# Transfers of an attention stage: from a written order with short lead to the scheduler's order with longer lead

## The chip, the cores and the metric

The kernel runs on one core of one Trainium2 chip. The metric is the device time of one execution in microseconds; the median over several runs is compared. TensorE is called PE, VectorE DVE, ScalarE ACT, GpSimd POOL, SyncE SP. Almost all transfers are issued from SP's queue.

## What is computed

One inference step of an encoder layer, for 1024 frames of a new stream and 32 frames of a running one with 512 cached frames (1056 token columns, model width 1024, 16 heads of 64). The reference, cut to its core:

```python
h = rmsnorm(x, norm_g)
q = rmsnorm(h @ Wq per head, q_g) * 64 ** -0.5
k = rmsnorm(h @ Wk per head, k_g);  v = h @ Wv
logf = log_sigmoid(h @ Wf + b_f);   C = cumsum(logf)
o = softmax(causal(q k^T + C[t] - C[s])) v            # per head
u = (h @ Wua) * sigmoid(h @ Wub);   conv = depthwise31(u) + b_dw
ya = (o * silu(h @ Wga)) @ w_pa
yb = (silu(layernorm(conv)) * silu(h @ Wgb)) @ w_pb
y = x + (sigmoid(h @ Wma) * ya + sigmoid(h @ Wmb) * yb) @ w_out
```

All data are 32-bit floats. Products are made in three passes over a high and a low part of each operand.

## The kernel before

**Stages.** The kernel runs through four stages. The opening transposes and scales the tokens (`x_split`) while it makes the first projection. The projections follow: V, the conv input `u`, keys and queries, and the gates `ga`; their results go to scratch tensors in device memory (`s_q`, `s_k`, `s_v`, `s_ga`, ...). Then comes the attention, head by head, and last the three output projections.

**A projection's weights** come as raw tiles of 512 KB in batches of two (`Batch`). The planner `begin` starts at the first product of a batch and puts its jobs on a list by steps; a step (`beat`) is one k-tile of a product, three matmuls. Jobs: the squares of the raw tile (`stage`, L117), the sum over partitions (`total`), the power of two to scale by (`power`), the high part by ACT (`split`) and the low part by DVE (`rest`, tile `wl`, L141). The next batch's raw tiles are loaded by `after.load` (L109), at steps 17 and 27. The raw tiles have four buffers, so a load waits until DVE has read the tile that lay there.

**The opening.** `x_split(0, ...)` goes over eight k-tiles: transposes on PE (L573), high part by ACT, low part by DVE (`xl`, L576), then the jobs listed for that k-tile, then the products of the two first weights, which lag behind (`drain`). `total(2)` sums the squares of the second weight on PE (L477) after its squares on ACT (`top(1)`, L596); `known(1)` makes its scale, `high(1, 0)` and `low(1, 0)` split its first third. `rooted(2, 3)` makes the square roots for tokens of tiles 2 to 4.

**The attention.** The list `seq` holds 16 heads of eight query blocks each, and four `Sample` entries for the running stream. At turn n of the loop over `seq`, PE makes the scores of block n + 3 (`start`, L1094 and L1095), transposes the softmax of block n (`turn`, L1119), goes four steps further in the remaining gate projections (`fill`, matmuls at L183 into `pj`, evicted by ACT into one of three tiles `t`, L932, and stored, L933), and makes the values of block n - 2. A head's values are made once, at its last block (L1138). Between are DVE (mask, maximum), ACT (exponential) and POOL (division). Conv taps of the last two channel groups run on DVE meanwhile.

**A head's operands.** `Head.load` issues eight transfers into QB, KB, QA and KA (L948 to L955), two buffers each, 1.5 MB in all. `Head.load_v` (L962) loads V, 256 KB, one buffer. Head 0 is loaded during the last gate projections ahead of the attention. In the loop the load of a head stands where its first block is five entries ahead, so two turns ahead of its first scores; V stands behind the values of the head before, which is the last reader of the one buffer.

**What sets the order.** Under `tc.manual_schedule` the engines named in it run their instructions as written; the others are ordered by a scheduler at build time, from a simulated timeline. In the opening and the projections PE, DVE and ACT follow the written order and SP doesn't. In the attention it is PE and SP (L986), in the last stage PE alone at first. Each engine's queue is in order: an instruction that waits holds up what is behind it.

Of the kernel before, what the change touches and what calls it, by code (L numbers as in the profile page):

```python
# [8 lines left out]
F32 = mybir.dt.float32  # L9
# [13 lines left out]
H = 16  # L23
# [30 lines left out]
def build(tc, xT, xt, wv, wf, ckT, cv, clT, stT, vec, cst, yT, kT, vO, lfO, cpT, csT):  # L54
# [4 lines left out]
    def pool(name, bufs=1, stack=es, **kw):  # L59
        return stack.enter_context(tc.tile_pool(name=name, bufs=bufs, reuse_waits="tile", **kw))  # L60
# [29 lines left out]
    class Batch:  # L90
# [31 lines left out]
        def total(self):  # L122
            pool, tag = totals[-1]
            self.ps = pool.tile([128, 512], F32, name="tot", tag=tag)
            if self.n == 2:
                nc.tensor.matmul(self.ps[:, :2], ones_b, self.topb, start=True, stop=True)
            else:
                for i in range(2):
                    nc.tensor.matmul(self.ps[:, 0:1], ones_b, self.topb[:, i:i + 1], start=(i == 0), stop=(i == 1))
# [7 lines left out]
        def high(self, i, wh, raw, ks):  # L137
            nc.scalar.mul(wh[:, ks, :], raw[:, ks, :], self.s[:, i:i + 1])  # L138

        def low(self, i, wl, wh, raw, ks):  # L140
            nc.vector.scalar_tensor_tensor(wl[:, ks, :], raw[:, ks, :], self.s[:, i:i + 1], wh[:, ks, :],  # L141
                                           op0=ALU.mult, op1=ALU.subtract)
# [78 lines left out]
    def begin():  # L221

        if not plan:
            return
        b = plan.pop(0)
        after = plan[0] if plan else None
        t = pace["tick"]
        jobs = [(25, b.total), (27, b.power)]
        if b.n == 2:
            jobs += [(3, lambda: b.stage(0)), (13, lambda: b.stage(1))]  # L230
            for i, n in ((0, 29), (1, 39)):
                jobs.append((n, lambda i=i: b.split(i)))
                jobs += [(n + 1 + 2 * p, lambda i=i, p=p: b.rest(i, p)) for p in range(3)]
        else:
            jobs += [(3 + 10 * i, lambda i=i: b.stage(i)) for i in range(2)]
            jobs.append((29, lambda: split.__setitem__(b.keys[0], split_v(b.keys[0][1], b))))
        if after:
            jobs += [(17 + 10 * i, after.load) for i in range(after.n)]
        prep.extend((t + n, fn) for n, fn in sorted(jobs, key=lambda e: e[0]))

    def steps(key, rh, rl, pspool, evac):
# [38 lines left out]
    class Banks:  # L280

        n = 0
# [157 lines left out]
    E = mybir.EngineType  # L440
# [72 lines left out]
    def squares(t, act=True, sl=slice(0, D), acc=None):  # L513
        r = rows(t)
        acc = rs9[:r, t:t + 1] if acc is None else acc
        sq = xip.tile([128, D], F32, name="sq", tag="sq", bufs=2)[:r, sl]
        x = xtok[t][:r, sl]
        if act:
            nc.scalar.activation(sq, x, AF.Square, accum_out=acc)
        else:  # L520
            nc.vector.scalar_tensor_tensor(sq, x, 1.0, x, op0=ALU.mult, op1=ALU.mult, accum_out=acc)

    def root(t0, nt):

        rs = rs9[:, t0:t0 + nt]
        v, y = [xip.tile([128, 4], F32, name=f"n4{i}", tag=f"n4{i}", bufs=2)[:, :nt] for i in range(2)]
        nc.vector.tensor_scalar(v, rs, 1.0 / D, EPS, op0=ALU.mult, op1=ALU.add)
        nc.scalar.activation(y, v, AF.Ln)
        nc.scalar.activation(y, y, AF.Exp, scale=-0.5)
        return lambda: newton(rs, v, y)  # L530

    def scale(t, h, pool=False):
        r = rows(t)
        x, f = xtok[t][:r, half[h]], rs9[:r, t:t + 1]
        if pool:
            nc.gpsimd.tensor_scalar(x, x, f, 1.0, op0=ALU.mult, op1=ALU.mult)
        else:
            nc.vector.tensor_scalar(x, x, f, None, op0=ALU.mult)
# [60 lines left out]
    def known(i):  # L599
        recs[i].power(psq[:, i + 1:i + 2], 1)  # L600
# [23 lines left out]
    def rooted(t0, nt):  # L624
        steps_of[t0] = root(t0, nt)
# [12 lines left out]
    for f in range(8):  # L638
# [14 lines left out]
    x_split(0, ws0, u0, {  # L653
        0: [lambda: top(1), lambda: squares(2, False)],
        1: [lambda: squares(3)],
        2: [lambda: total(2), lambda: high(0, 1), lambda: low(0, 1)],
        3: [lambda: known(1), lambda: squares(4, False), lambda: high(1, 0), lambda: low(1, 0)],
        4: [lambda: rooted(2, 3), lambda: high(0, 2)],
        5: [lambda: steps_of[2](), lambda: scale(2, 0), lambda: scale(3, 0, True), lambda: scale(4, 0), lambda: low(0, 2)],
        6: [lambda: scale(3, 1, True), lambda: scale(2, 1), lambda: high(1, 1), lambda: low(1, 1)],  # L660
        7: [lambda: scale(4, 1), lambda: high(1, 2), lambda: low(1, 2)]})
# [38 lines left out]
    def split_v(c, rec):  # L700
        wh2, wl2, raws2 = [], [], rec.raws
        for raw in raws2:
            with tc.high_priority(offset=1500):
                wh, wl = [vp.tile([128, 4, VC], F16, name=a, tag=a, bufs=4) for a in ("vwh", "vwl")]
                rec.high(0, wh, raw, slice(0, 4))
                for k in (0, 2):
                    rec.low(0, wl, wh, raw, slice(k, k + 2))
            wh2.append(wh)
            wl2.append(wl)

        def running():
            ps = pj.tile([128, 512], F32, name="pjs", tag="pj")
            for n in range(2):
                for j in range(4):
                    nc.tensor.matmul(ps[32 * j:32 * j + 32, :VC], xsm[:, 2 * j + n, :],
                                     raws2[j // 2][:, (2 * j + n) % 4, :], start=(n == 0), stop=(n == 1))
            pace["credit"] -= 1.3
            later(4, lambda: gathered(ps))

        def gathered(ps):  # L720
            v4 = vp.tile([TS, 4, VC], F32, name="v4", tag="v4", bufs=1)
            for j in range(4):
                nc.scalar.copy(v4[:, j, :], ps[32 * j:32 * j + 32, :VC])
            vs = vp.tile([TS, VC], F32, name="vs", tag="vs", bufs=1)
            nc.vector.tensor_reduce(vs, v4.rearrange("p j n -> p n j"), axis=AX.X, op=ALU.add)
            nc.vector.tensor_copy(z[:TS, 8, 4 * c:4 * c + 4], vs[:, 256:])
            nc.sync.dma_start(vO[T:, 256 * c:256 * c + 256], vs[:, :256])
            nc.sync.dma_start(s_vs[:, 256 * c:256 * c + 256], vs[:, :256])

        later(14, running)  # L730
        return wh2, wl2, rec.inv
# [4 lines left out]
    for c in range(4):  # L736
# [13 lines left out]
        pace["rate"] = R_V  # L750
        wh2, wl2, inv = split.pop(("v", c))
        begin()
        for t in range(8):
            ps = pj.tile([128, 512], F32, name="pjv", tag="pj")
            n = 0
# [181 lines left out]
    class Head:  # L937
# [20 lines left out]

        def load_v(self):
            h = self.h  # L960
            self.V = hp.tile([128, 8, 64], F32, name="V", tag="V", bufs=1)
            nc.sync.dma_start(self.V, s_v[:, :, 64 * h:64 * h + 64].rearrange("b t d -> t b d"))  # L962

    pace["rate"] = R_U
# [3 lines left out]
    hp = pool("hp", 2, stack=p2, side="right")  # L968
    heads = [Head(h) for h in range(H)]
# [13 lines left out]


    pe = ExitStack()
    pe.enter_context(tc.manual_schedule(engines={E.PE, E.SP}))  # L986
    pace["rate"], pace["credit"] = R_A, 0.0
    taps.extend(sums(7))
    psS = pool("psS", 2, stack=p2, space=PS)
# [11 lines left out]
    def fill(n):  # L1001
        for _ in range(n):
            next(flow, None)
# [145 lines left out]
    seq = []  # L1149
# [5 lines left out]
    def start(b):  # L1155
        if getattr(b, "i", 1) == 0:
            h = b.head
            if h.h % 2 == 0:
                h.ot = heads[h.h + 1].ot = ap.tile([128, T], F32, name="ot", tag="ot", bufs=2)
        b.scores()  # L1160

    def pending(b):
        return isinstance(b, Sample) or b.i % 2
# [36 lines left out]
    ln = layernorm()  # L1200
    sides["shift"] = ap.tile([128, TT], F32, name="shift", bufs=1)
    nc.sync.dma_start(sides["shift"], s_m)
    start(seq[0])
    fill(8)
    start(seq[1])
# [2 lines left out]
    for n, b in enumerate(seq):  # L1208
        if n + 3 < len(seq):
            start(seq[n + 3])  # L1210
        if n + 5 < len(seq) and getattr(seq[n + 5], "i", 1) == 0:
            seq[n + 5].head.load()
        if n + 6 < len(seq) and isinstance(seq[n + 6], Sample):
            seq[n + 6].load()
        if isinstance(b, Sample):
            fill(4)
            b.turn()
        else:
            b.turn()
            fill(4 if b.i > 2 or b.head.h != 8 else 0)  # L1220
        if n >= 2 and pending(seq[n - 2]):
            seq[n - 2].values()
        if n >= 3 and isinstance(seq[n - 3], Sample):
            seq[n - 3].finish()
        if n >= 2 and getattr(seq[n - 2], "i", 0) == 7 and seq[n - 2].head.h + 1 < H:
            heads[seq[n - 2].head.h + 1].load_v()
        if "ready" in sides:
            next(ln, None)
    for b in seq[-2:]:
# [6 lines left out]
    pe = ExitStack()  # L1236
# [9 lines left out]
    class Banks3:  # L1246
        n = 0
# [383 lines left out]
```

## Time and profile before

| | us |
|---|---|
| median of 3 runs | 1451.53 |
| lowest to highest | 1445.54 to 1453.81 |
| profiled execution | 1445.9 |
| its span, first to last instruction | 1443.9 |

| engine | busy us | share of the span |
|---|---|---|
| PE | 1347.8 | 93% |
| DVE | 976.5 | 68% |
| ACT | 723.0 | 50% |
| POOL | 496.5 | 34% |

The mean granted clock of TensorE is 0.969. The stages lie about at 0 to 60 us (opening), 60 to 560 (projections), 560 to 1160 (attention) and 1160 to 1444 (output projections). Busy shares are averages over these stages; a stage's own limit is read from its rows. In a row of waits stand the total, the number and the longest, in microseconds; in a row of the timeline the start, the length, the engine, the line, and in brackets the idle time before and what ended it.

### The profile page before, as it was taken

Reading aid. Unit: us, or ns where it says so; the run is one execution under the profiler, and the core shown is the slowest. Engines: PE = TensorE matmul, PEld = TensorE weight load, DVE = VectorE, ACT = ScalarE, POOL = GpSimd, SP = SyncE. Lnnn points to the kernel's source line nnn. Section 1 sums busy time; section 2 is a strip of 40 time slices with the busy share of each in tenths; the row PEclk is TensorE's granted clock in tenths of the full one; section 3 lists DMA queues with packets and bytes.
Section 4 is the critical chain, followed back from the end, with each engine's and each line's share of the span. In section 5 each row is a group of like instructions: output and inputs, shape, how many; then the busy total and the mean of one; then the engine's idle time right before and its main releaser. Section 6 shows DMA issues by size and latency. Waiting matters only on the chain.

```text
span 1443.9 us, 24762 instructions
## 1 busy us (share of the span) xinstructions
PE 1347.8 (93%) x9383; PEld 1020.0 (71%) x9383; DVE 976.5 (68%) x1534; ACT 723.0 (50%) x1360; POOL 496.5 (34%) x548
## 2 busy tenths in 40 slices
PE   8999999999999999787989788978888999999999
PEld 5687866666666666565666566656665689999999
DVE  6787888869798988656767645544444459455664
ACT  6544547575768535444544454534543465423321
POOL 2000126265748302333333322211211228545653
PEclk9999999999999999999999999999999999999999
DMA  6242434373435232335343543453444197743462
GB/s 233 92 148 85 125 89 130 109 195 116 131 121 168 100 128 95 99 102 148 108 130 107 155 116 83 121 149 88 116 116 124 49 359 258 233 135 120 144 202 73
DMA packets 113495, 194.96 MB, mean 135 GB/s; under 512 B 34080, under 2 KB 80032, under 8 KB 113376
## 3 DMA queue, kind: packets, MB, share of 16 engines
q1 hardware_dynamic: 113232, 193.31, 43.9%
q8 instruction: 74, 1.21, 0.4%
q14 instruction: 45, 0.37, 0.1%
q10 hardware_dynamic: 144, 0.07, 0.0%
HBM read 127.68 MB, written 65.64 MB: 134 GB/s over the span
## 4 chain that ended last, share of the span: by engine, by line
PE 71%; DMA 10%; DVE 5%; SPq 5%; ACT 4%; issue 3%; POOL 1%; ACTq 0%; DVEq 0%; POOLq 0%
PE pj L183 47%; PE pjv L760 6%; PE pj L1463 5%; PE po L1138 5%; DMA KA<-s_ak 5%; PE ptr L1119 3%; DMA raw<-wf 2%; DMA KA<-s_k 2%; PE psS L1095 1%; DVE y L368 1%; PE psS L1094 1%; ACT t L932 1%; DVE nm L1099 1%; DVE wl L141 1%; ACT P L1102 1%
## 5 line engine op out<-in xcount | busy, mean ns | idle before, releaser
L183 PE MATMUL pj<-xh,wh 128*128 128x352 f16 (+2 forms) x1536 | 489.0, 318 | 8.2 <-ACT t L932 6.9
L183 PE MATMUL pj<-xh,wl 128*128 128x352 f16 (+2 forms) x1536 | 488.1, 318 | 0.7 <-DVE wl L141 0.6
L183 PE MATMUL pj<-xl,wh 128*128 128x352 f16 (+2 forms) x1536 | 487.5, 317 | 0.1
L183 PEld LDWEIGHTS <-wh 128*128 128x128 f16 x3072 | 305.4, 99 | 165.4 <-issue 2.6
L368 DVE SCALAR_TENSOR_TENSOR y<-u,vec_t,y 128x1086 f32<-128x1086 f32 x240 | 342.6, 1428 | 9.5 <-ACT y L365 6.6
L1105 POOL TENSOR_SCALAR P<-P,nm 128x128 f32<-128x128 f32 (+7 forms) x128 | 119.1, 931 | 336.7 <-DVE nm L1104 281.7
L183 PEld LDWEIGHTS <-wl 128*128 128x128 f16 x1536 | 152.6, 99 | 84.4 <-issue 10.7
L141 DVE SCALAR_TENSOR_TENSOR wl<-raw,sc,wh 128x384 f16<-128x384 f32 (+1 forms) x192 | 119.1, 655 | 30.5 <-ACT wh L138 30.5
L1122 ACT COPY pt<-ptr 128x512 f32<-128x512 f32 (+3 forms) x128 | 64.4, 503 | 143.9 <-PE ptr L1119 143.3
L1102 ACT ACTIVATE P<-psS,nm 128x128 f32<-128x128 f32 (+7 forms) x128 | 94.8, 741 | 65.5 <-DVE nm L1099 52.0
L1094 PE MATMUL psS<-KB,QB 128*128 128x256 f32 (+2 forms) x192 | 82.7, 432 | 39.7 <-DMA KB<-s_k 33.8
L1097 DVE TENSOR_TENSOR psS<-psS,cmask 128x128 f32<-128x128 f32 x128 | 37.7, 295 | 118.2 <-PE psS L1095 117.7
L1099 DVE TENSOR_REDUCE nm<-psS 128x1 f32<-128x128 f32 (+7 forms) x128 | 96.3, 754 | 8.5 <-DVE psS L1097 0.5
L1095 PE MATMUL psS<-KA,QA 68*128 68x256 f32 (+2 forms) x192 | 70.1, 366 | 30.1 <-DMA KA<-s_ak 24.6
L1119 PE MATMUL ptr<-ident,P 128*128 128x128 f32 x576 | 93.6, 294 | 1.2 <-ACT pt L1122 1.2
L175 POOL TENSOR_TENSOR wl<-raw,wh 128x384 fp32r<-128x384 f32 (+1 forms) x51 | 63.4, 1271 | 74.6 <-ACT wh L172 58.7
L1119 PEld LDWEIGHTS ptr<-ident,P 128*128 128x128 f32 x576 | 77.2, 153 | 6.9 <-ACT pt L1122 1.5
L1094 PEld LDWEIGHTS psS<-KB,QB 128*128 128x128 f32 x192 | 37.5, 195 | 57.3 <-issue 39.9
L138 ACT ACTIVATE wh<-raw,sc 128x1024 f16<-128x1024 f32 (+1 forms) x68 | 72.7, 1089 | 7.8 <-DVE sc L158 7.5
L869 POOL TENSOR_TENSOR sql<-sqf,sqh 128x352 fp32r<-128x352 f32 x48 | 58.7, 1224 | 50.7 <-ACT sqh L866 50.6
L1138 PE MATMUL po<-pt,V 128*64 128x256 f32 x640 | 72.8, 382 | 0.3 <-ACT pts L1051 0.3
L117 ACT ACTIVATE junk<-raw 128x1024 bf16<-128x1024 f32 x62 | 65.2, 1052 | 12.9 <-DMA raw<-wf 12.8
(271 smaller groups left out, 2574.8 us busy)
## 6 DMA issues: line engine op xcount, KB each, us to landing
raw<-wf SPq DMA_DIRECT2D x92, 512.0 KB
QB<-s_q SPq DMA_DIRECT2D x32, 256.0 KB
KB<-s_k SPq DMA_DIRECT2D x32, 256.0 KB
kT<-qn SPq DMA_DIRECT2D x8, 528.0 KB
s_ga<-t SPq DMA_DIRECT2D x24, 176.0 KB
s_gb<-t SPq DMA_DIRECT2D x24, 176.0 KB
s_ma<-t SPq DMA_DIRECT2D x24, 176.0 KB
s_mb<-t SPq DMA_DIRECT2D x24, 176.0 KB
```

Source lines behind the costliest of these rows:

```text
L138: nc.scalar.mul(wh[:, ks, :], raw[:, ks, :], self.s[:, i:i + 1])
L141: nc.vector.scalar_tensor_tensor(wl[:, ks, :], raw[:, ks, :], self.s[:, i:i + 1], wh[:, ks, :], op0=ALU.mult, op1=ALU.subtract)
L183: nc.tensor.matmul(ps, a[:, kt, :], b(kt, sl), start=(first and n == 0), stop=(last and n == N - 1))
L368: t = nc.vector.scalar_tensor_tensor(y, u[:, i:i + CW], w, y, op0=ALU.mult, op1=ALU.add)
L760: nc.tensor.matmul(ps[:, :VC], a, b, start=(n == 0), stop=(n == 23))
L1094: nc.tensor.matmul(ps[:, b, :wm], QB[:, qsl], KB[:, ksl], start=True, stop=False)
L1095: nc.tensor.matmul(ps[:, b, :wm], QA[:, qsl], KA[:, ksl], start=False, stop=True)
L1099: nc.vector.tensor_reduce(nm[:, 0:1], ps[:, :nb, :w], axis=AX.XY, op=ALU.max, negate=True)
L1102: nc.scalar.activation(P[:, :nk].rearrange("p (b w) -> p b w", b=nb), ps[:, :nb, :w], AF.Exp, bias=nm[:, 0:1], accum_out=nm[:, 1:2])
L1105: nc.gpsimd.tensor_scalar(P[:, :nk], P[:, :nk], nm[:, 2:3], 1.0, op0=ALU.mult, op1=ALU.mult)
L1119: nc.tensor.transpose(pt[:, 128 * j:128 * j + 128], P[:, 128 * (4 * u + j):128 * (4 * u + j) + 128], ident)
L1138: nc.tensor.matmul(po[rows], V[:, j, :], parts[c][:, j, :], start=(c % 2 == 0 and j < 2), stop=(c % 2 == 1 and j >= 2 * c))
```

## The change

Five edits. SP leaves the written order in the attention. A head's queries and keys are loaded nine entries ahead of its first block, with head 1's ahead of the first block of all. V has two buffers, and the next head's V is loaded at block 3. The next batch's raw weights are listed at steps 5 and 15. In the opening, the sum of the second weight's squares moves from k-tile 2 to 3, its scale and first split from 3 to 4, behind the square roots.

```diff
@@ begin
-            jobs += [(17 + 10 * i, after.load) for i in range(after.n)]
+            jobs += [(5 + 10 * i, after.load) for i in range(after.n)]
@@ x_split(0, ...)
-        2: [lambda: total(2), lambda: high(0, 1), lambda: low(0, 1)],
-        3: [lambda: known(1), lambda: squares(4, False), lambda: high(1, 0), lambda: low(1, 0)],
-        4: [lambda: rooted(2, 3), lambda: high(0, 2)],
+        2: [lambda: high(0, 1), lambda: low(0, 1)],
+        3: [lambda: total(2), lambda: squares(4, False)],
+        4: [lambda: known(1), lambda: rooted(2, 3), lambda: high(1, 0), lambda: low(1, 0), lambda: high(0, 2)],
@@ Head.load_v
-            self.V = hp.tile([128, 8, 64], F32, name="V", tag="V", bufs=1)
+            self.V = hp.tile([128, 8, 64], F32, name="V", tag="V", bufs=2)
@@ attention
-    pe.enter_context(tc.manual_schedule(engines={E.PE, E.SP}))
+    pe.enter_context(tc.manual_schedule(engines={E.PE}))
...
+    heads[1].load()
     start(seq[0])
...
-        if n + 5 < len(seq) and getattr(seq[n + 5], "i", 1) == 0:
-            seq[n + 5].head.load()
+        if n + 9 < len(seq) and getattr(seq[n + 9], "i", 1) == 0:
+            seq[n + 9].head.load()
         if n + 6 < len(seq) and isinstance(seq[n + 6], Sample):
             seq[n + 6].load()
+        if getattr(b, "i", 0) == 3 and b.head.h + 1 < H:
+            heads[b.head.h + 1].load_v()
...
-        if n >= 2 and getattr(seq[n - 2], "i", 0) == 7 and seq[n - 2].head.h + 1 < H:
-            heads[seq[n - 2].head.h + 1].load_v()
```

## The prediction

> **What bounds the kernel now.** I read the page first: its span and the chain of work that ended last.
>
> ```profile
> span 1443.9 us, 24762 instructions
> PE 71%; DMA 10%; DVE 5%; SPq 5%; ACT 4%; issue 3%; POOL 1%; ACTq 0%; DVEq 0%; POOLq 0%
> ```
>
> TensorE carries the chain, but a tenth of it is transfers. The view of busy time by stretches says in which stage: opening, projections, attention, output projections. Columns: stretch, length, busy time (count) of PE, PEld, DVE, ACT and POOL, granted clock, DMA share, GB/s.
>
> ```profile
> 0.00:60.00 60.00, 53.61 (x327) 35.00 (x328) 42.07 (x102) 36.44 (x70) 9.38 (x19) 0.94 0.50 182
> 60.00:560.00 500.00, 493.87 (x3544) 342.20 (x3542) 419.61 (x494) 295.63 (x548) 193.65 (x191) 1.00 0.39 125
> 560.00:1160.00 600.00, 520.99 (x3604) 368.87 (x3602) 339.00 (x715) 282.11 (x598) 146.95 (x221) 0.93 0.42 112
> 1160.00:1444.00 284.00, 279.38 (x1915) 273.90 (x1913) 175.79 (x225) 108.83 (x146) 146.55 (x117) 1.00 0.58 190
> ```
>
> PE stands idle 79.0 us of the 600 in the attention, and only there and in the opening is its clock below 1.00. The projections leave 6.1 us idle in 500, the last stage 4.6 in 284. So the attention decides. The view of waits, PE alone, from 560 to 1160 us (total, times, longest):
>
> ```profile
> PE psS L1094 <- DMA KB<-s_k: 33.8, 10, 5.2
> PE psS L1095 <- DMA KA<-s_ak: 24.6, 11, 2.9
> PE pj L183 <- ACT t L932: 6.9, 10, 2.0
> PE psS L1095 <- DMA KA<-s_k: 5.4, 3, 1.9
> PE psS L1094 <- issue: 2.4, 1, 2.4
> PE psS L1094 <- ACT P L1102: 2.3, 3, 1.0
> PE ptr L1119 <- ACT pt L1122: 1.2, 1, 1.2
> ```
>
> The first score of a head waits for that head's keys: 33.8 + 24.6 + 5.4 = 63.8 us, and 66.2 with the 2.4 us at the same line whose cause isn't shown. All other waits together are some 12 us. The timeline of SP's queue and of PE at one head's start shows how:
>
> ```profile
> 1093.00 0.47 SPq L948 DMA_DIRECT2D QB<-s_q  x1
> 1098.44 0.48 SPq L955 DMA_DIRECT2D KA<-s_ak  x1
> 1102.90 0.55 PE L1094 MATMUL psS<-KB,QB 128*128 128x256 f32 x1 [4.92 <-DMA KB<-s_k]
> 1105.40 0.55 PE L1095 MATMUL psS<-KA,QA 68*128 68x256 f32 x1 [1.95 <-DMA KA<-s_k]
> ```
>
> PE had asked for the keys at 1102.90 - 4.92 = 1097.98, only 5.0 us after the first of the head's eight loads was issued; the last landed 12.4 us after it. The issue is late because the text puts it late: SP follows the written order, and the loads stand two block turns ahead of the head's first scores.
>
> **The clock behind the wait.** The same head in stretches:
>
> ```profile
> 1097.70:1102.90 5.20, 0.28 (x2) 0.03 (x1) 0.16 (x1) 1.37 (x3) 1.12 (x1) 0.91 1.04 219
> 1102.90:1105.40 2.50, 0.55 (x1) 0.29 (x2) 0.00 (x0) 0.00 (x0) 0.00 (x0) 0.50 1.04 243
> 1105.40:1108.60 3.20, 3.20 (x13) 2.43 (x14) 1.18 (x4) 0.95 (x3) 0.37 (x1) 0.50 0.85 233
> 1108.60:1112.00 3.40, 3.40 (x34) 2.04 (x33) 0.95 (x3) 0.45 (x1) 0.42 (x1) 0.97 0.01 5
> ```
>
> After the idle stretch PE works 3.2 us at clock 0.50: 1.6 us lost a second time. And the trace holds a head that hardly waited, beside one that did:
>
> ```profile
> 729.50:765.10 35.60, 30.48 (x200) 21.72 (x199) 23.80 (x46) 17.86 (x37) 9.46 (x13) 0.90 0.44 118
> 765.10:794.00 28.90, 27.76 (x199) 20.21 (x199) 21.68 (x38) 13.36 (x31) 10.12 (x13) 1.00 0.47 125
> ```
>
> Same matmuls, 35.60 against 28.90 us. Of the 6.7 us, 5.12 - 1.14 = 4.0 are less idleness and 30.48 - 27.76 = 2.7 are faster matmuls. So a head without the stall takes some 29 us, and at that rate no other engine has yet shown itself to be late.
>
> **The change, part by part.**
>
> *Queries and keys nine blocks ahead.* Four turns earlier than now: the last block of the head before and blocks 0 to 2, about half a head, 14 us at 28.9 us a head (an estimate, four of eight turns). The lead grows from 5.0 to about 19 us against the 12.4 needed: 6.6 us to spare. The two buffers allow it: those for head h were last read by block 7's scores of head h-2, issued three turns ahead of the new place. Head 1 is loaded before the first block. So 66.2 us go.
>
> *The clock.* Bounds: the attention's row gives (1 - 0.93) x 600 = 42 us lost, and by the stretches above half of that lies in work, not idleness (3.2 x 0.50 + 3.4 x 0.03 = 1.7 against 5.2 x 0.09 + 2.5 x 0.50 = 1.7), so 21 us; the pair of heads gives 2.7 us each, 35 us for the 13 large stalls that I count in PE's timeline. I take 26.
>
> The Trainium skill, "TensorE: Matmul & The Clock Gate", Part 1, says that the gate knows only half and full speed and needs some 3.4 us of sustained work to open; by it 13 stalls would cost 13 x 1.7 = 22 us. This trace agrees with the 0.50 and, within its 3.2 us, with the time.
>
> *SP in the scheduler's order.* Only PE's order stays written. The stage ahead of the attention has SP in this mode already, and there the scheduler moves loads up as far as data and buffers allow: head 0's load is written among the `ga` gates, whose stores begin at 493.3 us, and was issued at 308.51.
>
> ```profile
> L933 SPq DMA_DIRECT2D s_ga<-t x24: 319/320/942, 493.3 to 574.4; - x24
> 308.51 0.51 SPq L948 DMA_DIRECT2D QB<-s_q  x1
> SPq L109 <- DVE wl L141: 89.3, 31, 14.0
> SPq L109 <- DVE wl L141: 120.4, 33, 28.9
> PE pst L877 <- POOL sql L869: 5.5, 5, 1.6
> ```
>
> So loads will be issued no later than where they are written, perhaps as soon as the buffer is free. The cost is in rows three and four (SP's waits at 60 to 560 us, and in the whole run): the scheduler queues a raw weight load while DVE still reads its buffer, and SP stands there, 3.6 us in the mean (120.4 / 33), and with it every load and store queued behind. In the projections that cost PE nothing: its largest wait there, row five, is for another engine. In the attention a gate's store may be held up so; three `t` tiles and chunks of eight fill steps (two turns, 28.9 / 4 = 7.2 us) let one be 14.4 us late, its own landing included. At best the 6.9 us of waits for ACT's `t` go; at worst, 30 us are added. With heads shorter by a fifth the 12 us of other waits may grow too. Together I take 10 us of new waits, nearer to nothing, because the mean wait of 3.6 us is far below both margins (6.6 and 14.4).
>
> The Trainium skill, "DMA: Bandwidth & Descriptors", section "Queues, rings and completion order", says that each DMA engine takes one queue's descriptors in ring order, which speaks against the change: a store issued behind a head's eight loads waits for them wherever they stand. No row here separates that from SP's own waits; by it the 6.9 us of `pj <- ACT t` would stay, as they do in my sum.
>
> *Two V buffers, V from block 3 on.* V is first read by block 7's values. PE has no wait for V in the rows above, so nothing is gained; 256 KB merely move. If its cover went, it would show as a wait at L1138.
>
> *Raw weights 12 steps earlier.* ACT's first reading of them waits now, but PE has no wait on weights in the attention, nothing to gain but ACT's slack:
>
> ```profile
> ACT junk L117 <- DMA raw<-wf: 12.8, 11, 2.7
> ```
>
> In the projections SP is already free to hoist, so the text's place changes little: 0, between -2 and +2 us of the 6.1 idle.
>
> *The opening sum.* Today PE waits at the total of the second weight's squares:
>
> ```profile
> 11.87 0.38 PE L477 MATMUL pj<-tops,ones_w 128*128 128x1 f32 x2 [1.81 <-ACT junk L596]
> 22.37 0.55 PE L573 MATMUL ptx<-ident,xtok 128*128 128x128 f32 x3 [1.76 <-DVE xl L576]
> ACT n L528 <- DVE n L527: 1.9, 2, 1.2
> ```
>
> Moved behind the next transposes, it lets the first product start once its own operands are there, 0.4 us sooner or so; with `known(1)` and the first weight split behind the square roots, DVE reaches the roots earlier, and 1.2 us of ACT's wait for them (row three) can shrink. But the second weight is ready later, and the later gap (row two) is set by DVE. Between 1 us lost and 2 us gained; I take 1 us gained.
>
> **The sum.** The profiled execution took 1445.9 us, its span 1443.9. 1445.9 - 66.2 - 26 - 1 + 10 = 1362.7. The median of the runs is 5.6 us above the profiled one; with that, 1368 us.
>
> **The rivals.**
>
> *Loads held up by raw weights (half the gain).* If SP stands at a raw load for more than the 6.6 us to spare in front of a head's loads, the stall returns by the excess; the longest such wait in the projections was 14.0 us, worth a full stall of 7.4. If half of the heads meet it, (66.2 + 26) / 2 = 46 us come back: about 1414. For: 31 such waits in 500 us. Against: their mean, and that the scheduler may issue the head's loads long before.
>
> *DVE becomes the bound.* Heads 1 to 6 still carry conv taps; the quickest holds 21.68 us of DVE work in 28.90, or 75%, the one before it 23.80. If 75% is the most that DVE sustains between its waits, such heads stay at 23.80 / 0.75 = 31.7 instead of 28.9: 2.8 x 6 = 17 us, 1385. It is inside the range and counted with the forecast.
>
> *Slower: stores behind raw weights stop the gates.* The gates' matmuls have one PSUM bank and three `t` tiles. If SP stands at each of the 22 raw loads for W us with a gate's store behind, PE loses W - 14.4 each time. It outweighs the 83 us gained from W = 18.2; at 20 us it is 22 x 5.6 = 123 us, 1491. For: one wait of 28.9 us in the whole run. Against: a mean of 3.6, and projections with PE 99% busy in the same mode.
>
> *It doesn't do what it says.* The scheduler might put the head loads behind other work, so that they land as late as now: 1450.
>
> **How the numbers follow.** Forecast 0.75 (with the DVE case), half the gain 0.12, no change 0.05, slower 0.08. The low end takes the upper clock bound, no new waits and 2 us in the opening: 1445.9 - 66.2 - 35 - 2 + 5.6 = 1348. The high end reaches to the half-gain case, 1415, and leaves out 0.13 above. The measurement of this kernel can tell about 0.5% from no change, 7 us: faster 0.87, same 0.05, slower 0.08.
>
> **What would show it.** Right: the waits of psS for KB and KA gone or below 10 us in total, the attention's clock at 0.98 or more, heads of 28 to 30 us, a head's QB issued a half to a whole head ahead of its first scores, and new waits of SP at L109 for `wl` inside the attention. Wrong: waits of `pj` for ACT's `t` in the tens, SP standing over 15 us at a raw load, psS waiting for ACT's exponentials, or KA loads that still land after PE asks.

## The result and the profile after

The changed kernel takes 1376.1 us (median of 4 runs, 1374.1 to 1378.1) against 1450.0 for the kernel before (median of 4 runs of this comparison): a ratio of 0.949, 95% interval 0.946 to 0.953. The forecast was 1368, the range 1348 to 1415. The profiled execution took 1377.2 us.

The page of the changed kernel, span, PE and the chain that ended last:

```profile
span 1375.1 us, 24786 instructions
PE 1326.3 (96%) x9383; PEld 1007.7 (73%) x9383; DVE 977.7 (71%) x1534; ACT 721.2 (52%) x1360; POOL 502.3 (37%) x548
PE 79%; DVE 8%; ACT 4%; DMA 4%; issue 3%; POOL 1%; SPq 0%; ACTq 0%; DVEq 0%; POOLq 0%
```

Transfers have fallen from 10% of the chain to 4%, SP's queue from 5% to nothing. PE's busy time is 21.5 us shorter with the same 9383 matmuls. The same piece of work, from the attention's first score to its last, as one stretch of the kernel before; the columns are the stretch, its length, busy time and instructions of PE, PEld, DVE, ACT and POOL, the granted clock, the DMA share and GB/s:

```profile
573.50:1136.90 563.40, 484.39 (x3342) 344.11 (x3341) 317.59 (x686) 269.51 (x578) 139.90 (x214) 0.93 0.43 114
```

And as one stretch of the changed kernel:

```profile
575.80:1068.60 492.80, 460.81 (x3343) 330.53 (x3341) 317.53 (x686) 266.64 (x578) 145.18 (x214) 0.98 0.45 125
```

The piece is 70.6 us shorter: PE's idleness fell from 79.0 to 32.0 us (47.0), its busy time by 23.6 us at a clock of 0.98 instead of 0.93. What lies ahead of it is 2.3 us longer, what lies behind 0.5 us shorter (307.0 and 306.5): 68.8 in all. PE's waits in the attention of the changed kernel (sum in us, count, longest):

```profile
PE pj L183 <- ACT t L932: 15.3, 18, 4.0
PE psS L1094 <- ACT P L1102: 12.7, 7, 4.9
PE psS L1027 <- ACT P L1102: 2.0, 2, 1.8
PE ptr L1119 <- ACT pt L1122: 1.5, 1, 1.5
```

No wait for keys is left. In their place stand 31.5 us of waits for ACT, where 12 us of other waits were before. Two of SP's own waits from 540 to 1110 us of the changed kernel:

```profile
SPq L948 <- PE psS L1095: 41.7, 13, 6.6
SPq L109 <- DVE wl L141: 26.0, 10, 5.8
```

And one head's loads in SP's timeline there:

```profile
597.16 0.45 SPq L948 DMA_DIRECT2D QB<-s_q  x1
601.68 0.52 SPq L955 DMA_DIRECT2D KA<-s_ak  x1
```

The first row of the waits says how the scheduler orders the loads: 13 of the 16 heads' first loads stand at the head of SP's queue until PE has made the last scores that read the buffer. The two rows of the timeline are the load of head 2, issued behind head 0's last scores and 36.7 us ahead of head 2's own first score at 633.84 us. Over heads 2 to 15 this lead is 30 to 40 us.

### The profile page after: what moved, and what is told of

The parts are those of the page before. It is cut to its first block, busy times and chain, and to the rows that moved or that the text cites. A ratio compares the mean times of both kernels' runs of the same rounds, so it can differ in the third digit from the quotient of the medians.

```text
span 1375.1 us, 24786 instructions
## 1 busy us (share of the span) xinstructions
PE 1326.3 (96%) x9383; PEld 1007.7 (73%) x9383; DVE 977.7 (71%) x1534; ACT 721.2 (52%) x1360; POOL 502.3 (37%) x548
## 4 chain that ended last, share of the span: by engine, by line
PE 79%; DVE 8%; ACT 4%; DMA 4%; issue 3%; POOL 1%; SPq 0%; ACTq 0%; DVEq 0%; POOLq 0%
PE pj L183 54%; PE pjv L760 6%; PE pj L1464 5%; PE po L1138 4%; PE ptr L1119 3%; DMA raw<-wf 2%; DVE y L368 2%; PE psS L1094 2%; DVE wl L141 2%; DVE nm L1099 2%; PE psS L1095 2%; ACT P L1102 1%; ACT t L932 1%; PE pst L877 1%; POOL sql L869 1%
## 5 line engine op out<-in xcount | busy, mean ns | idle before, releaser
L183 PE MATMUL pj<-xh,wh 128*128 128x352 f16 (+2 forms) x1536 | 484.8, 316 | 18.9 <-ACT t L932 15.3
L1105 POOL TENSOR_SCALAR P<-P,nm 128x128 f32<-128x128 f32 (+7 forms) x128 | 122.8, 961 | 271.5 <-DVE nm L1104 237.5
L1094 PE MATMUL psS<-KB,QB 128*128 128x256 f32 (+2 forms) x192 | 82.6, 431 | 12.8 <-ACT P L1102 12.7
L1119 PE MATMUL ptr<-ident,P 128*128 128x128 f32 x576 | 85.5, 275 | 1.5 <-ACT pt L1122 1.5
L117 ACT ACTIVATE junk<-raw 128x1024 bf16<-128x1024 f32 x62 | 65.2, 1052 | 33.5 <-DMA raw<-wf 33.4
L1119 PEld LDWEIGHTS ptr<-ident,P 128*128 128x128 f32 x576 | 70.0, 142 | 7.7 <-POOL topb L120 1.7
L120 POOL CAST topb<-tops 128x2 bf16<-128x2 f32 x35 | 13.4, 383 | 167.8 <-ACT junk L117 117.7
L1104 DVE RECIPROCAL nm<-nm 128x1 f32<-128x1 f32 x128 | 20.6, 161 | 74.1 <-ACT P L1102 73.0
```

Source lines behind the costliest of these rows:

```text
L183: nc.tensor.matmul(ps, a[:, kt, :], b(kt, sl), start=(first and n == 0), stop=(last and n == N - 1))
L1094: nc.tensor.matmul(ps[:, b, :wm], QB[:, qsl], KB[:, ksl], start=True, stop=False)
L1105: nc.gpsimd.tensor_scalar(P[:, :nk], P[:, :nk], nm[:, 2:3], 1.0, op0=ALU.mult, op1=ALU.mult)
L1119: nc.tensor.transpose(pt[:, 128 * j:128 * j + 128], P[:, 128 * (4 * u + j):128 * (4 * u + j) + 128], ident)
```

## Experiments

Ratios are to the kernel before in the same comparison. Its median was 1443.8 to 1445.8 us in these, so kernels of different comparisons are compared by their ratios.

**Scheduler's order alone.**

```diff
-    pe.enter_context(tc.manual_schedule(engines={E.PE, E.SP}))
+    pe.enter_context(tc.manual_schedule(engines={E.PE}))
```

> The kernel before with one edit: SP leaves the written order in the attention (loads still written five entries ahead, one V buffer, weights at steps 17 and 27). Theory A (the scheduler issues a head's loads when its buffer comes free, wherever they are written; in the trace after, 13 of 16 first loads wait for scores of the head before last): nearly the whole gain, 1365 to 1390 us, no wait of psS for KB or KA. Theory B (the place in the text decides): 1440 to 1455 us, with the psS waits for keys still at 50 to 66 us.

Measured: 1374.8 us, ratio 0.951 (0.949 to 0.953). No wait for keys; the waits for ACT are those of the full change:

```profile
PE pj L183 <- ACT t L932: 15.1, 17, 3.9
PE psS L1094 <- ACT P L1102: 13.0, 8, 5.1
```

This one edit gives the whole gain. Under the scheduler, five or nine in the text can't be told apart: here too the loads of heads 2 to 15 are issued 30 to 40 us ahead.

**Nine ahead alone, SP in the written order.**

```diff
+    heads[1].load()
     start(seq[0])
...
-        if n + 5 < len(seq) and getattr(seq[n + 5], "i", 1) == 0:
-            seq[n + 5].head.load()
+        if n + 9 < len(seq) and getattr(seq[n + 9], "i", 1) == 0:
+            seq[n + 9].head.load()
```

> The kernel before with queries and keys written nine entries ahead and head 1's ahead of the first block; SP keeps the written order, all else as before. Theory A (lead alone brings the gain): 1360 to 1385 us, psS waits for keys under 5 us. Theory B (the scheduler's order is needed, the written queue holds the loads up behind stores): 1400 to 1450 us.

Measured: 1369.7 us, ratio 0.949 (0.946 to 0.951); no wait for keys. The load of head 2, from SP's timeline, and its first score, from PE's, without a wait before it:

```profile
607.42 0.46 SPq L948 DMA_DIRECT2D QB<-s_q  x1
627.54 0.40 PE L1094 MATMUL psS<-KB,QB 128*128 128x256 f32 x1
```

For heads 2 to 15 the lead is 20 to 26 us. So each of the two edits suffices, and the longer lead is what they have in common. The waits for ACT are here too, 15.8 us for `t` and 8.2 us for `P`, so most of them don't come from SP's order.

**A lead in between.** Six instead of five entries ahead, nothing else.

```diff
-        if n + 5 < len(seq) and getattr(seq[n + 5], "i", 1) == 0:
-            seq[n + 5].head.load()
+        if n + 6 < len(seq) and getattr(seq[n + 6], "i", 1) == 0:
+            seq[n + 6].head.load()
```

> The kernel before with queries and keys written six entries ahead instead of five, SP in written order. One turn is some 3.6 us, so the lead grows from 5.0 to 8.6 us against the 12.4 needed. Lead theory: about half of the stall stays, psS waits for keys 25 to 40 us, and the clock recovers by less than half since a shorter stall may still halve it: 1405 to 1425 us. If the stall were set by bandwidth and not by the lead, the waits would stay at 60 us and the time at 1445.

Measured: 1416.6 us, ratio 0.980 (0.978 to 0.982). PE's waits in its view of waits:

```profile
PE psS L1095 <- DMA KA<-s_ak: 16.1, 8, 2.6
PE psS L1094 <- DMA KB<-s_k: 15.9, 6, 3.6
PE psS L1095 <- DMA KA<-s_k: 5.9, 4, 2.0
PE psS L1094 <- issue: 3.7, 1, 3.7
```

The three rows for keys are 37.9 us, in the range of the lead theory. With the row whose cause isn't shown it is 41.6 us instead of 66.2: one turn of lead took away 24.6 us, and the time followed. By the other theory of the expectation, a bound by bandwidth, the waits would have stayed.

**The opening undone in the changed kernel.**

```diff
-        2: [lambda: high(0, 1), lambda: low(0, 1)],
-        3: [lambda: total(2), lambda: squares(4, False)],
-        4: [lambda: known(1), lambda: rooted(2, 3), lambda: high(1, 0), lambda: low(1, 0), lambda: high(0, 2)],
+        2: [lambda: total(2), lambda: high(0, 1), lambda: low(0, 1)],
+        3: [lambda: known(1), lambda: squares(4, False), lambda: high(1, 0), lambda: low(1, 0)],
+        4: [lambda: rooted(2, 3), lambda: high(0, 2)],
```

> The changed kernel with the opening's sum, scale and split back at k-tiles 2 and 3. If moving it was worth the 1 us of the prediction, the opening's wait of 1.8 us at the total is back and the time is 1 us more; by the trace after (start of the transposes of the third chunk at 34.50 against 34.36) it is worth nothing, within 0.3 us at that point. The whole time stays at 1370 to 1380 us. If the 3 us lost between 58 and 73 us came from that edit, the first V product starts at 73 again instead of 76.

Measured: 1376.7 us, ratio 0.951 (0.949 to 0.954), which can't be told from the change. The wait of 1.81 us at the total is back, and the transposes of the third chunk start at 34.46 us, so moving the sum was worth nothing. The first V product starts at 76.3 us with and without it, so the 3 us in front of it aren't this edit's.

**ACT's squares held.** In the changed kernel ACT often stands at the squares of a raw weight that hasn't landed, in all 33.4 us where it was 12.8 before. The row of ACT's waits in the changed kernel:

```profile
ACT junk L117 <- DMA raw<-wf: 33.4, 16, 4.6
```

One such place in its timeline (start, duration, engine, line, operation, and in brackets the wait before it): SP issues two weights behind a head's eight loads, ACT stands at the first for 4.45 us, the exponential behind it comes late, and PE waits 4.94 us for the score bank that it frees.

```profile
602.29 2.89 SPq L109 DMA_DIRECT2D raw<-wf  x2
608.43 1.06 ACT L117 ACTIVATE junk<-raw 128x1024 bf16<-128x1024 f32 x1 [4.45 <-DMA raw<-wf]
609.92 0.36 ACT L1102 ACTIVATE P<-psS,nm 128x128 f32<-128x128 f32 x1
610.42 0.69 PE L1094 MATMUL psS<-KB,QB 128*128 128x384 f32 x1 [4.94 <-ACT P L1102]
```

ACT's order is the scheduler's, from a simulated timeline; presumably the weight lands sooner in it, which no run here shows. The edit keeps (its lines are shortened) the squares behind the exponential that the text has last before them:

```diff
+            with (tc.issue_after(sides["exp"].ins) if "exp" in sides else ExitStack()):
                 nc.scalar.activation(junk[...], raw..., AF.Square, accum_out=self.tops[:, i:i + 1])
...
-                nc.scalar.activation(P[...], ps[...], AF.Exp, ...)
+                sides["exp"] = nc.scalar.activation(P[...], ps[...], AF.Exp, ...)
```

> The changed kernel with ACT's squares of a raw weight tile held, in the attention, behind the exponential written last before them, so that the scheduler can't put them earlier into ACT's queue. Theory C (most of the 31.5 us that PE now waits for ACT comes from ACT standing at squares whose weights haven't landed, 33.4 us in 16 waits, with exponentials and evictions behind): ACT's wait for raw under 10 us, PE's waits for ACT at 10 to 18 us, 1352 to 1367 us. Theory D (they come from the denser queues of DVE and ACT at a head of 29 us): PE's waits stay at 25 to 35 us, 1370 to 1380 us.

Measured: 1357.1 us, ratio 0.939 (0.937 to 0.941). No wait of ACT for a raw weight of this kind is left. PE's waits in the attention:

```profile
PE pj L183 <- ACT t L932: 14.5, 19, 2.4
PE psS L1094 <- ACT P L1102: 5.9, 4, 2.6
PE po L1138 <- ACT pts L1051: 2.5, 1, 2.5
PE psS L1027 <- ACT P L1102: 1.5, 2, 1.2
```

The same piece of work as one stretch of this kernel, in the columns above:

```profile
572.50:1050.30 477.80, 453.08 (x3343) 327.68 (x3341) 316.87 (x686) 269.69 (x581) 143.32 (x215) 0.99 0.47 129
```

From the first score to the last it takes 477.8 us against 492.8: idleness fell by 7.3 us (32.0 to 24.7), busy time by 7.7, since the long waits went and with them the slow matmuls behind them. The time is as theory C had it. The waits fell to 24.4 us only, not to the 10 to 18 expected, and the longest from 4.9 to 2.6 us. So theory C holds for the long waits and not for the many short ones.

**Raw weights at steps 17 and 27 in the changed kernel.**

```diff
-            jobs += [(5 + 10 * i, after.load) for i in range(after.n)]
+            jobs += [(17 + 10 * i, after.load) for i in range(after.n)]
```

> The changed kernel with the raw weights listed at steps 17 and 27 again. With SP in the scheduler's order the place in the text should not matter, as for the heads' loads: 1372 to 1380 us, ACT's wait for raw at 28 to 38 us. If the place matters, later loads make ACT wait longer, 45 us or more, and the time 1380 to 1390.

Measured: 1373.0 us, ratio 0.950 (0.948 to 0.953), ACT's wait for raw 34.5 us. The place in the text doesn't matter.

**One V buffer at the old place in the changed kernel.**

```diff
-            self.V = hp.tile([128, 8, 64], F32, name="V", tag="V", bufs=2)
+            self.V = hp.tile([128, 8, 64], F32, name="V", tag="V", bufs=1)
...
-        if getattr(b, "i", 0) == 3 and b.head.h + 1 < H:
-            heads[b.head.h + 1].load_v()
...
+        if n >= 2 and getattr(seq[n - 2], "i", 0) == 7 and seq[n - 2].head.h + 1 < H:
+            heads[seq[n - 2].head.h + 1].load_v()
```

> The changed kernel with one V buffer, and V written behind the values of the head before, as before the change. No PE wait named V in the trace before or after, and the scheduler's order alone, with one V buffer, took 1374.8: so 1370 to 1382 us and no wait at the values' line. A rival, that the second buffer frees PE of a wait at the head's end, would show 4 us or more per head there, 1430.

Measured: 1375.4 us, ratio 0.952 (0.949 to 0.954), no wait for V. It is worth nothing here. One wait of 3.1 us, at head 4's first score, is put down to QB, though that load had been issued 36.9 us ahead; in the changed kernel PE waits 2.66 us at the same place for ACT's `P`.

**Nine ahead in the written order, with the squares held.**

Both edits are those shown above, in the kernel before.

> The kernel before with queries and keys nine entries ahead, SP in the written order (1369.7 us by itself), and ACT's squares held as in the run with the changed kernel. Written SP issues the raw weights one at a time at steps 17 and 27. Theory C: ACT's wait for raw falls from 27.5 us to under 6, PE's waits for ACT from 26 to 10 to 16, 1350 to 1362 us. Theory D: 1366 to 1375 us. It is also the candidate to beat both kernels.

Measured: 1358.7 us, ratio 0.940 (0.938 to 0.942), 11 us less than without the hold (by the ratios 12). No wait of ACT at L117 for `raw` is left. PE's waits for ACT in the attention are 12.5, 6.1 and 2.0 us, again above the 10 to 16 expected. It beats both kernels of the change and can't be told from the changed kernel with the squares held.

**What is left: a fourth `t`, and thinner taps.** Both start from the changed kernel with the squares held.

```diff
-            t = t352("t", 3)
+            t = t352("t", 4)
```

> The changed kernel with the squares held (1357.1 us), and four tiles t instead of three for the evicted gates. If what is left of PE's waits for ACT's t (14.5 us in 19) comes from ACT standing until an older store of t has landed, it falls to 8 to 11 us and the time to 1350 to 1355. If it comes from ACT being busy with squares and exponentials when a chunk ends, it stays at 13 to 15 us and the time within 2 us of 1357.

Measured: 1357.7 us, ratio 0.939 (0.937 to 0.941); PE's waits for `t` 12.4 us. A fourth tile brings nothing that can be told. The trace of the held kernel agrees: its largest wait of ACT at L932 for a store of `t` is one of 1.5 us.

```diff
-R_U, R_V, R_QK, R_G, R_A = 0.21, 0.18, 0.165, 0.23, 0.2
+R_U, R_V, R_QK, R_G, R_A = 0.21, 0.18, 0.165, 0.23, 0.17
```

> The changed kernel with the squares held, and the conv taps in the attention paced at 0.17 a step instead of 0.20, so that DVE has 15% fewer taps in each of the earlier heads and the same number in all. If the rest of PE's waits for ACT (24 us) comes from DVE's density in the heads with taps (theory D for the rest), it falls to 16 to 21 us and the time to 1349 to 1355; if not, it stays within 3 us of 24 and the time within 2 us of 1357.

Measured: 1354.1 us, ratio 0.937 (0.935 to 0.938), the fastest of all; PE's waits for ACT are 12.8 and 6.4 us, 19.2 together. The waits fell by 5.2 us, as expected if they come from DVE's density; that fits, but one profile of each doesn't show it. The 3 us lie within the intervals of the two kernels (0.937 to 0.941 and 0.935 to 0.938), so the gain over the held kernel isn't settled.

## Why the prediction was right, point by point

*The bound and its cause.* Right. The waits for keys are gone to the last one, 66.2 us, and the run with six entries shows that they followed the lead. Of the signs named, four came: no wait for keys, a clock of 0.98, loads a head ahead, SP's waits for `wl`. Heads took 31.3 us in the mean (1 to 14), not 28 to 30. And two of the signs of being wrong came as well: 15.3 us of waits of `pj` for `t`, and 12.7 us of psS for ACT's exponentials.

*How the lead comes about.* The sum took half a head from the place in the text and left it open that the scheduler would load as soon as a buffer is free. It does, so the lead was 30 to 40 us and not about 19, and the margin of 6.6 us was never needed. The sentence "loads will be issued no later than where they are written" held. The sizing itself is borne out by nine alone in the written order, where the lead is 20 to 26 us and was enough too.

*The clock.* 26 us taken, 23.6 measured on the same piece of work; with nine alone, which has no wait above 2.6 us in the attention, it is 29.8 us (454.55 us of busy PE). The price of the stalls was sized well; the new waits gave some of it back, 7.7 us by the run with the squares held.

*New waits.* Here the sum was off: 10 us taken, 31.5 - 12.0 = 19.5 measured, inside its bounds of -7 and 30. The mechanism that I priced, SP standing at raw weights before DVE had read the buffer, did appear (26.0 us in 10 waits, 5.8 at most), and hurt nothing that the trace shows: no wait for keys, and in the attention ACT stood 0.6 us in all, once, for a store of `t`. SP stood longer still at the loads of V, 54.2 us in 14 waits, 12.4 at most, which the sum didn't name and which cost as little. What cost time was one queue further. ACT's wait for raw weights was in the quoted rows (12.8 us), and I read it as slack of ACT's. But ACT's queue is in order and holds the exponentials and evictions that PE needs; the same kind of wait grew to 33.4 us (it is 19.5 with six entries and 27.5 with nine alone). That a shorter head leaves ACT less slack would explain the growth, but no run takes that apart from the order of the queues. With the squares held the attention is 15.0 us shorter. Of the remaining 24 us the runs settle only that a fourth `t` doesn't remove them.

*The opening.* 1 us taken, 0.1 us lost up to the third chunk (34.50 against 34.36). PE's longest waits in the opening behind its first matmul, in the timeline after:

```profile
10.87 0.27 PE L183 MATMUL pj<-xh,wh 128*128 128x256 f16 x1 [0.77 <-ACT xh L575]
18.07 0.39 PE L183 MATMUL pj<-xh,wh 128*128 128x256 f16 x1 [2.44 <-ACT wh L138]
34.50 0.72 PE L573 MATMUL ptx<-ident,xtok 128*128 128x128 f32 x4 [0.50 <-DVE xl L576]
```

And the opening after as one stretch, in the columns above:

```profile
0.00:60.00 60.00, 54.22 (x326) 35.49 (x327) 42.05 (x102) 35.84 (x68) 8.33 (x19) 0.91 0.49 180
```

The wait at the total is gone as said, and the second weight, ready later, cost 2.44 us at 18.07. PE's idleness in these 60 us fell by 0.6 us, from 6.4 to 5.8, and its busy time rose by as much, at a clock of 0.91 instead of 0.94, a term that the sum left out here.

*V and the raw weights' steps.* Nothing, as said: the two runs that undo them can't be told from the change.

*The rivals.* Half the gain and slower both needed SP to stand at raw weights for longer than 6.6 or 18 us; in the attention its longest wait there was 5.8. DVE as the bound had 31.7 us for the heads with taps, and heads 1 to 6 did take 31.5 in the mean. But heads 7 to 14, by which the conv taps were all but done, took 31.2, with DVE busy 57% of the time instead of 77%, and no wait of PE in the attention names DVE. So the taps don't account for it. The rule quoted from the Trainium skill, "DMA: Bandwidth & Descriptors", "Queues, rings and completion order", would delay whatever is issued behind a head's loads. The raw weight that landed late at 608.4 us had been issued right behind them, which agrees. But the DMA engines were busy 99% of the time from 598 to 608 us, so it may as well be the bandwidth that they share; no run took the two apart. PE's waits for `t`, which by that rule would stay at 6.9 us, grew to 15.3.

*The sum.* -66.2 - 23.6 + 19.5 gives -70.3 in the attention, where 70.6 was measured; the forecast had -82.2. The whole forecast for the profiled execution was 83.2 us less, and it became 68.7 (1445.9 to 1377.2): 14.5 us were missing. In the attention 11.6 of them lie, mostly the new waits. Ahead of it 2.3 us were lost where 1 was to be gained; they hold 3 us at the first V product that belong to no edit (below). Behind it 0.5 us were gained. That the median missed by only 8 us is luck. The forecast added 5.6 us because the median before lay that far above the profiled execution; the median after lies 1.1 us below it.

## What to carry to other kernels

A load's place in the text is only its lead if the issuing queue follows the text; first see which engines are ordered by whom, then compare the lead, in microseconds, with the time from first issue to last landing. When a stall is removed, look at the waits of every in-order queue that feeds the bound engine, also those that cost nothing now: a wait that was hidden by the stall comes to light in its place. A scheduler that goes by simulated times can put an instruction ahead of data that lands late. Holding back what wasn't urgent was worth 15 us here in the changed kernel and 11 with nine alone.

## What the runs showed of the hardware

A wait of 2.0 us in PE, where it is 0.7 at other times, came with a loss of 3 us in two profiles, the changed kernel's and that with the opening undone. It stands between 58 and 73 us, in front of the first V product. In the changed kernel a POOL cast of 128 x 2 elements took 1.07 us instead of 0.19 in the kernel before, PE waited 2.02 us for it instead of 0.67, and its clock then fell. The stretch from 64 to 70 us of the kernel before:

```profile
64.00:70.00 6.00, 6.00 (x45) 3.80 (x46) 5.40 (x7) 1.62 (x2) 0.00 (x0) 1.00 0.00 0
```

And of the changed kernel:

```profile
64.00:70.00 6.00, 6.00 (x31) 3.42 (x29) 4.80 (x7) 2.22 (x4) 0.00 (x0) 0.72 0.01 3
```

The V products by tile, with their first and last start, in the changed kernel:

```profile
L760 PE MATMUL pjv<-vwh,xh x256: 271/274/285, 76.3 to 186.7; 128*128 128x260 f16 x128
```

And in the changed kernel with ACT's squares held, which is the same text up to the attention:

```profile
L760 PE MATMUL pjv<-vwh,xh x256: 271/274/285, 73.1 to 183.4; 128*128 128x260 f16 x128
```

31 matmuls instead of 45 in the same 6 us. Profiles with the text of before up to the attention start V at 73.2 to 75.6 us, those with the text of after at 73.0 to 76.3, so the 3 us come and go without any of the edits. Nor does the wait always lower the clock. It is 2.02 us in three more profiles (scheduler's order alone, six entries, one V buffer), but there the clock from 64 to 70 us is 1.00 and V starts at 75.6, 74.4 and 74.5. Why POOL's cast is slow at times, and why the clock falls after some of these waits only, stays open.
